# Router logits from the residual rows, two transposes in one go, VectorE for the first expert's low halves, and the first 256 tokens' branches inside the attention loop

## The chip, the cores and the metric

The kernel runs on one core of one Trainium2 chip. The metric is the device time of one execution in microseconds. Three executions of the kernel before took 3333.39, 3338.21 and 3341.09 us, median 3338.21 us. Line numbers of the kernel before are written as L and a number.

## The reference

One layer of an encoder for 2048 tokens of 1024 features, all in float32:

```
h   = rmsnorm(x, norm1_g);  P = h @ w_in           # columns: RWKV | attention q,k,v | two gates
y_A = RWKV7(forward + backward scan)               # 8 heads of 64, group norm, bonus term, times g
y_B = dilated window attention                     # 3 groups of 4 heads (dilation 1, 4, 16)
      # the groups are merged: o = sum_g softmax_g(lse) * o_g
x   = x + (sigmoid(g_A) * (y_A @ w_rwkv_out) + sigmoid(g_B) * (y_B @ w_attn_out)) @ w_out
h2  = rmsnorm(x, norm2_g)                          # x * rsqrt(mean(x*x) + eps) * norm2_g
grp = argmax(h2 @ w_router_group + b_router_group) # 4 groups of 8 experts
top 2 of (h2 @ w_router_expert + b_router_expert) inside grp; gate = p(grp) * softmax(top 2)
x   = x + sum over the 2 experts of gate * (silu(h2 @ w_gate) * (h2 @ w_up)) @ w_down
```

## The kernel before

The work is one straight program, in stages: projections; RWKV scans beside the rest of the projections; the windowed attention; a loop over eight blocks of 256 tokens that merges the two branches, projects, norms and routes; then the 32 experts; then a loop for what overflows an expert's slots. A framework plans the order of the instructions on each engine ahead of time, from its own estimates: work that stands earlier in the program goes first where it is ready, and later work fills gaps. On the chip each engine, and each queue of transfers, then runs its list strictly in that order. Tiles with one tag in a pool share that tag's buffers in turn, in program order; a pool that is closed gives its memory to the next.

Exact float32 products are made of two parts: a tile is split into a rounded high half (ScalarE copies it to `fp32r`) and the remainder (a subtraction), and three matmuls combine the halves (`PASS`).

**Attention** (L885 to L962). Three head groups, each with 16 tiles of 128 tokens, in the order 2, 1, 0. In a block of 2 or 4 tiles, q and k are loaded (`qkr`), transposed by TensorE into the PSUM tag `tq` of two banks, and copied out by VectorE (`KK`) and ScalarE (`QZ`). For each tile follow the scores (`s`), VectorE's mask and maximum (`sm`, `ob`), ScalarE's exponentials, a transpose (`pt`), the product with v (`po`) and a store of unnormed rows with their maxima and sums into the scratch tensor `o_d`. Each tile of groups 1 and 0 also advances `weights()`, which splits the weights of the next stage.

**Between** (L967 to L1036). Nine loads of constants into the pool `w5`: `gnB`, `g2`, `gup`, the router's weights `wr` (36 columns, in runs of 4 and 32 values) and biases `br`. Then `rwkv(0, psC, "tq")`. `rwkv(q)` finishes the RWKV branch of 256 tokens: it loads two scans' rows (`y0`, `y1`) and sums them, group norms them on VectorE, adds the bonus term with two steps on GpSimd (L1022, L1023), multiplies by the gate (two matmuls into PSUM, L1028, L1029), and `split_T` (L985 to L987) transposes the result and splits it to `yT`. It has three yields. Its PSUM tiles are those of the tag it is given.

**The block loop** (L1212 to L1246). `attn(q)` merges the three groups' rows: three loads of `oc` from `o_d`, small steps for the softmax over groups, a weighted sum (L1139 to L1141), `split_T` to `oT`. `attn(0)` stands ahead of the loop and takes its buffers from the pool `y5`, which opens after the attention's pools are closed. For each block q, `merge` runs 8 times (18 matmuls each into one of two banks `ab`, the gates `tg` loaded from scratch, a product on VectorE, then GpSimd and ScalarE); `residual` runs four times (two tiles of 128 tokens, two halves of 512 columns, 24 matmuls each into `px`); `norm2` squares on ScalarE, takes the inverse root with eleven small VectorE steps and scales (L1186); `logits` turns and multiplies for the router. The next block's `rwkv` and `attn` are advanced between these steps, with the PSUM tag `t5` of two banks. The second tile's logits and the routing (`tail`) are advanced in the next block, after merges 1, 3 and 5 and later.

`logits(h2, lg)` transposes four times into `th` (one bank), copies, runs four matmuls into `pl` (one bank), and then does all that again; between the halves it yields. `route` (L1056 to L1114) finds the group and the two experts, ranks the tokens of each expert and adds them to the table `ts`.

**The way to the experts** (L1248 to L1298). After the last block's routing, the experts are sorted by load (`order`), matmuls give the index tables (`IDX1`, `IDX2`), the pools are closed, and `load_gu(0, G)` loads the first expert's four pieces of 1 MB; `piece` lets ScalarE copy each half (L1288) and here GpSimd subtract (L1289), for all other experts VectorE. Then GpSimd gathers the first expert's rows (L1378).

Of the kernel before, what the change touches and what calls it, by code (L numbers as in the profile page):

```python
# [42 lines left out]
def hybrid_layer_kernel(ctx, tc, x, positions, norm1_g, w_in, mu_prev, mu_next, w_decay0, w_decay_up, a_gate0,  # L43
# [838 lines left out]
    made = 0  # L882
    wA, wB, wO = [], [], []
    parts_of_weights = weights()
    for g in (2, 1, 0):  # L885
# [4 lines left out]
        for i0 in range(0, NT, nb):  # L890
# [18 lines left out]
            for i in range(i0, i0 + nb):  # L909
# [57 lines left out]
    gnB = mk(w5, [128, 2, HD], F32, "gnB")  # L967
    nc.sync.dma_start(gnB[:, 0], gn_w[0:1, :].to_broadcast([128, HD]))
    nc.sync.dma_start(gnB[:, 1], gn_b[0:1, :].to_broadcast([128, HD]))
    g2 = mk(w5, [128, D], F32, "g2")  # L970
    nc.sync.dma_start(g2, norm2_g[0:1, :].to_broadcast([128, D]))
    gup = mk(w5, [128, HD], F32, "gup")
    nc.sync.dma_start(gup, g_up[0])
    wr = mk(w5, [128, KT, 36], F32, "wr")
    nc.sync.dma_start(wr[:, :, 0:4], w_router_group[0].rearrange("(k p) e -> p k e", p=128))
    nc.sync.dma_start(wr[:, :, 4:36], w_router_expert[0].rearrange("(k p) e -> p k e", p=128))
    br = mk(w5, [128, 36], F32, "br")
    nc.sync.dma_start(br[:, 0:4], b_router_group[0:1, :].to_broadcast([128, 4]))
    nc.sync.dma_start(br[:, 4:36], b_router_expert[0:1, :].to_broadcast([128, 32]))
    def split_T(dst, src, nk, ps, tag):  # L980

        for k in range(nk):
            pt = mk(ps, [128, 256], F32, tag)
            for j in range(2):
                PE.transpose(pt[:, j * 128:(j + 1) * 128], src[:, j, k * 128:(k + 1) * 128], ident)  # L985
            S.activation(dst[:, k, 0], pt, AF.Copy)
            V.tensor_tensor(dst[:, k, 1], pt, dst[:, k, 0], op=OP.subtract)  # L987

    def rwkv(q, ps, tag):

        tq = slice(q * 256, (q + 1) * 256)
        y0 = mk(yb, [128, 2, HD], F32, "y0")
        nc.sync.dma_start(y0, y_d[0, tq].rearrange("(j p) f -> p j f", p=128))
        y1 = mk(yb, [128, 2, HD], F32, "y1")
        nc.sync.dma_start(y1, y_d[1, tq].rearrange("(j p) f -> p j f", p=128))
        V.tensor_tensor(y0, y0, y1, op=OP.add)
        yh = y0.rearrange("p j (h n) -> p (j h) n", n=N)
        mu = mk(yb, [128, 16], F32, "mu")
        V.tensor_reduce(mu, yh, axis=AX.X, op=OP.add)
        V.tensor_scalar(mu, mu, 1.0 / N, None, op0=OP.mult)  # L1000
        V.tensor_tensor(yh, yh, mu[:, :, None].to_broadcast([128, 16, N]), op=OP.subtract)
        S.activation(y1, y0, AF.Square)
        yield
        V.tensor_reduce(mu, y1.rearrange("p j (h n) -> p (j h) n", n=N), axis=AX.X, op=OP.add)
        V.tensor_scalar(mu, mu, 1.0 / N, GN_EPS, op0=OP.mult, op1=OP.add)
        ri = mk(yb, [128, 16], F32, "ri5")
        rsqrt(yb, ri, mu, [128, 16], "rt5")
        V.tensor_tensor(yh, yh, ri[:, :, None].to_broadcast([128, 16, N]), op=OP.mult)
        V.tensor_tensor(y0, y0, gnB[:, 0, None, :].to_broadcast([128, 2, HD]), op=OP.mult)
        V.tensor_tensor(y0, y0, gnB[:, 1, None, :].to_broadcast([128, 2, HD]), op=OP.add)  # L1010
        yield
        vv = mk(yb, [128, 2, HD], F32, "y1")
        nc.sync.dma_start(vv, v_d[tq].rearrange("(j p) f -> p j f", p=128))
        vh = vv.rearrange("p j (h n) -> p j h n", n=N)
        bq = mk(yb, [2 * H, 256], F32, "bq")
        nc.sync.dma_start(bq, bon_d.rearrange("d h t -> (d h) t")[:, tq])
        pt = mk(ps, [128, 2, 2, H], F32, tag)
        for j in range(2):
            PE.transpose(pt[:, j].rearrange("p d h -> p (d h)"), bq[:, j * 128:(j + 1) * 128], ident[:2 * H, :2 * H])
        bsum = mk(yb, [128, 2, H], F32, "bsum")  # L1020
        V.tensor_reduce(bsum, pt.rearrange("p j d h -> p j h d"), axis=AX.X, op=OP.add)
        G.tensor_tensor(vh, vh, bsum[:, :, :, None].to_broadcast([128, 2, H, N]), op=OP.mult)  # L1022
        G.tensor_tensor(y0, y0, vv, op=OP.add)  # L1023
        sgt = mk(yb, [128, 256], F32, "sgt")
        nc.sync.dma_start(sgt, sg_d[:, tq])
        for j in range(2):
            pg = mk(ps, [128, HD], F32, tag)
            PE.matmul(pg, sgt[:, j * 128:(j + 1) * 128], gup, start=True, stop=True)  # L1028
            V.tensor_tensor(y0[:, j], y0[:, j], pg, op=OP.mult)  # L1029
        yield  # L1030
        yT = YT[q] = mk(yb, [128, 4, 2, 256], F32R, "yT")
        split_T(yT, y0, 4, ps, tag)

    YT, OT = {}, {}
    for _ in rwkv(0, psC, "tq"):
        pass  # L1036

    stC.close()

# [150 lines left out]
    def logits(h2, lg):  # L1190
        pl = mk(psE, [128, 36], F32, "pl", bufs=1)
        for k4 in range(2):
# [9 lines left out]
            if k4 == 0:  # L1202
                yield
# [8 lines left out]
    for _ in attn(0):  # L1212
        pass
# [382 lines left out]
```

## Time and profile before

| | |
|---|---|
| median of three runs | 3338.21 us |
| the profiled execution | 3351.28 us |
| its span, first to last instruction | 3349.6 us |
| mean granted clock of TensorE | 0.957 |
| attention | about 1820 to 2078 us |
| block loop, first merge to last residual | about 2079 to 2539 us |
| routing's end, index tables | about 2574 us |
| experts | about 2583 to 3336 us |

A row of a group of instructions gives line, engine, operation, output and input, count, then busy us, mean ns of one, and idle us of the engine ahead of them with what ended the idle time. A row of a timeline gives start and duration in us. PEld is TensorE's weight load, PEclk the granted clock as a share of full speed. TensorE's matmuls are pipelined, so their durations overlap.

### The profile page before, as it was taken

How to read it: one execution, taken by the hardware profiler on the slowest of the kernel's cores; microseconds unless marked ns; L12 is line 12 of the kernel's file. 1: busy time of each engine (PE TensorE's matmuls, PEld its weight loads, DVE VectorE, ACT ScalarE, POOL GpSimd, SP SyncE). 2: the span in 40 equal slices, each digit the busy share in tenths (PEclk: the TensorE clock that was granted, in tenths of full speed). 3: DMA queues.
4: the chain of work that ended last, by engine and by line, in shares of the span. 5: the costliest groups of instructions: out<-in, count | busy, mean ns of one | idle time of the engine just before them, and what ended most of it. 6: DMA issues, size and time to landing. Idle time of an engine off the chain costs nothing. (4 is left out here: it accounts for less than half of the span.)

```text
span 3349.6 us, 72079 instructions
## 1 busy us (share of the span) xinstructions
PE 3024.1 (90%) x29102; PEld 2466.8 (74%) x29102; DVE 2210.9 (66%) x4134; ACT 1522.0 (45%) x2913; POOL 544.8 (16%) x648
## 2 busy tenths in 40 slices
PE   6999978888989998898999987999996999999997
PEld 4888777667877787678877886778784667777775
DVE  5233368566766686648664776677774677888885
ACT  6333344453434434343433864111122566677764
POOL 0000012011112020112110000323233121222231
PEclk9899989999999999999999999999996999999999
DMA  7144365666545655565456654444433899999986
GB/s 280 60 136 137 98 208 194 211 199 206 161 150 174 201 167 160 166 199 162 145 172 184 182 174 144 129 130 144 127 120 115 286 308 323 337 336 341 330 295 201
DMA packets 361082, 652.63 MB, mean 195 GB/s; under 512 B 33717, under 2 KB 181765, under 8 KB 356522
## 3 DMA queue, kind: packets, MB, share of 16 engines
q1 hardware_dynamic: 338538, 599.61, 53.8%
q0 software_dynamic: 11104, 36.32, 4.4%
q10 hardware_dynamic: 11104, 12.06, 1.1%
q8 instruction: 230, 3.77, 0.5%
q14 instruction: 106, 0.87, 0.1%
HBM read 497.52 MB, written 153.10 MB: 194 GB/s over the span
## 5 line engine op out<-in xcount | busy, mean ns | idle before, releaser
L716 PE MATMUL dn<-wh,hk 128*128 128x256 f32 x3456 | 475.4, 295 | 24.0 <-DVE wh L659 9.4
L1289 DVE TENSOR_TENSOR wh<-raw,wh 128x1024 fp32r<-128x1024 f32 x376 | 441.4, 1219 | 80.1 <-ACT wh L1288 79.1
L716 PEld LDWEIGHTS dn<-wh,hk 128*128 128x128 f32 x3456 | 443.8, 200 | 42.5 <-DVE wh L659 11.1
L1288 ACT ACTIVATE wh<-raw 128x1024 fp32r<-128x1024 f32 x384 | 387.3, 1053 | 149.9 <-DMA raw<-in_w_down_dram 69.2
L720 PE MATMUL dn<-hk,wh 128*128 128x512 f32 x1536 | 404.1, 411 | 30.6 <-ACT gs L730 11.0
L1418 PE MATMUL pgu<-wh,xT 128*128 128x512 f32 x1536 | 377.7, 403 | 0.2 <-ACT xT L1393 0.2
L720 PEld LDWEIGHTS dn<-hk,wh 128*128 128x128 f32 x1536 | 284.5, 193 | 106.9 <-ACT gs L730 13.2
L1418 PEld LDWEIGHTS pgu<-wh,xT 128*128 128x128 f32 x1536 | 287.9, 190 | 78.1 <-issue 7.4
L280 PE MATMUL pp<-hq,wh 128*128 128x512 f32 x1008 | 254.0, 408 | 1.6 <-ACT hq L217 1.3
L280 PEld LDWEIGHTS pp<-hq,wh 128*128 128x128 f32 x1008 | 193.1, 194 | 48.0 <-ACT hq L217 2.3
L1174 PE MATMUL px<-w,mT 128*128 128x512 f32 x768 | 196.2, 406 | 0.0
L1462 PE MATMUL py<-wh,hT 128*128 128x512 f32 x768 | 191.4, 401 | 0.4 <-ACT hT L1440 0.4
L476 POOL TENSOR_TENSOR t<-t,ld 128x512 f32<-128x512 f32 x32 | 51.2, 1600 | 857.6 <-DVE t L465 483.9
L1174 PEld LDWEIGHTS px<-w,mT 128*128 128x128 f32 x768 | 142.8, 188 | 36.8 <-issue 3.4
L1462 PEld LDWEIGHTS py<-wh,hT 128*128 128x128 f32 x768 | 140.4, 188 | 33.1 <-issue 1.2
L1354 POOL DMA_INDIRECT out_dram<-ys,IDX x49 | 91.2, 1861 | 315.5 <-issue 105.5
L283 ACT ACTIVATE u<-pp 128x512 f32<-128x512 f32 x56 | 61.3, 1094 | 152.3 <-PE pp L280 125.3
L730 ACT ACTIVATE gs<-dn,drv 128x512 f32<-128x512 f32 x64 | 75.7, 1183 | 116.9 <-PE dn L720 80.5
L1158 PE MATMUL ab<-yT,w 128*128 128x256 f32 x768 | 114.4, 293 | 7.2 <-DVE tg L1161 3.6
L1378 POOL DMA_INDIRECT xg<-h_d,IDX x49 | 72.7, 1484 | 280.2 <-PE tx L1392 175.1
L1158 PEld LDWEIGHTS ab<-yT,w 128*128 128x128 f32 x768 | 99.5, 193 | 12.4 <-DVE tg L1161 5.6
L415 ACT ACTIVATE uv<-pre 32x512 f32<-32x512 f32 x128 | 75.2, 588 | 61.1 <-PE pre L409 59.9
(415 smaller groups left out, 5434.5 us busy)
## 6 DMA issues: line engine op xcount, KB each, us to landing
wh<-wc_d SPq DMA_DIRECT2D x204, 512.0 KB
raw<-in_w_gate_dram SPq DMA_DIRECT2D x64, 1024.0 KB
raw<-in_w_up_dram SPq DMA_DIRECT2D x64, 1024.0 KB
raw<-in_w_down_dram SPq DMA_DIRECT2D x64, 1024.0 KB
wc_d<-wh SPq DMA_DIRECT2D x68, 512.0 KB
ld<-rkk_d SPq DMA_DIRECT2D x192, 128.0 KB
raw<-in_w_in_dram SPq DMA_DIRECT2D x82, 256.0 KB
g_d<-gs SPq DMA_DIRECT2D x64, 256.0 KB
```

The source lines that it names most:

```text
L280: PE.matmul(pp, whs[k // 4][:, a, k % 4], hq[q][k // 2][:, k % 2, b], start=n == 0, stop=n == 3 * KT - 1)
L415: S.activation(uv[p * 64:p * 64 + 32, s::2].rearrange("p s (h e n) -> p s h e n", e=2, n=N)[:, :, :, e], pa[o:o + 32], AF.Copy)
L716: PE.matmul(pp[e][:, j * 256:(j + 1) * 256], lhs(2 * e + j, hk, k, a), wk_[:, b], start=k + j + m == 0, stop=k + j + m == KT + 2, skip_gro ...
L720: PE.matmul(pp[e], wk_[:, a, e * 128:e * 128 + 128], hk[k // 2][:, k % 2, b], start=k + m == 0, stop=k + m == KT + 1)
L730: S.activation(natural(gs), by_residue(pp[e]), AF.Tanh, scale=0.5, bias=DP[:, 38 + ct:39 + ct])
L1158: PE.matmul(pa[:, e], wt[k][:, a, cs_], src[:, k, b], start=e + n == 0, stop=n == 3 * nk - 1, skip_group_check=True)
L1174: PE.matmul(px, mT[k // 4][:, k % 4, a, j * 128:(j + 1) * 128], wO[k][:, b, fs], start=n == 0, stop=n == 3 * KT - 1)
L1288: S.activation(wh[:, 0, ks], raw[:, ks], AF.Copy)
L1289: eng.tensor_tensor(wh[:, 1, ks], raw[:, ks], wh[:, 0, ks], op=OP.subtract)
L1354: G.indirect_dma_start(out=x2_d, out_offset=bass.IndirectOffsetOnAxis(ap=idx, axis=0), in_=src, in_offset=None, bounds_check=T - 1, oob_is ...
L1418: PE.matmul(pgu[n], xT[:, x_, 4 * a + k], wh[:, w_, k], start=a + k + m == 0, stop=a + k + m == 6)
L1462: PE.matmul(py[f], hT[:, x_, 2 * a + k], wh[:, w_, k, f * 512:(f + 1) * 512], start=a + k + m == 0, stop=a + k + m == 4)
```

## The change

- The constants' loads, `split_T` and `rwkv` move ahead of the attention loop in the text. `wr` is multiplied by `norm2_g` once, with `norm2_g` loaded as `g2T` (1024 runs of one value).
- `rwkv(0)` and a new `attn0()` are advanced one step after each of the tiles 8 to 15 of the attention's last group. `attn0` does for 128 tokens at a time what `attn(0)` did for 256, in the buffers `y0` and `y1`; its transposes (`turn_o`) stay behind the attention.
- `logits` transposes `xr`, the residual rows, in two tiles of the tag `t5`, yields, and then runs the eight matmuls; the inverse root is multiplied in with the bias. The tag `th` is gone; `pl` has two banks.
- The first expert's subtractions are VectorE's.

```diff
+    wr = mk(w5, [128, KT, 36], F32, "wr")
...
+    g2T = mk(yb, [128, KT], F32, "bsum")
+    nc.sync.dma_start(g2T, norm2_g[0].rearrange("(k p) -> p k", p=128))
+    V.tensor_tensor(wr, wr, g2T[:, :, None].to_broadcast([128, KT, 36]), op=OP.mult)
...
+    def attn0():
+        for j in range(2):
+            oc = mk(yb, [128, 3, 264], F32, f"y{j}")
+            for g in range(3):
+                nc.sync.dma_start(oc[:, g], o_d[g, j * 128:(j + 1) * 128])
+            OC.append(oc)
+            yield
+            nm, sm = oc[:, :, 256:260], oc[:, :, 260:264]
+            mn = mk(yb, [128, 4], F32, "ri5")
...
+            V.tensor_tensor(og, og, wg[:, :, :, None].to_broadcast([128, 3, 4, N]), op=OP.mult)
+            V.tensor_tensor(oc[:, 0, 0:256], oc[:, 0, 0:256], oc[:, 1, 0:256], op=OP.add)
+            V.tensor_tensor(oc[:, 0, 0:256], oc[:, 0, 0:256], oc[:, 2, 0:256], op=OP.add)
+            yield
+    early = iter(())
     for g in (2, 1, 0):
...
                 if g < 2:
                     next(parts_of_weights, None)
+                if g == 0 and i >= 7:
+                    next(early, None)
+                    if i == 7:
+                        early = chain(rwkv(0, psC, "tq"), attn0())
...
-    for _ in rwkv(0, psC, "tq"):
+    for _ in early:
         pass
...
-        pr = mk(psE, [128, 2, 2, NE], F32, "pl", bufs=1)
+        pr = mk(psE, [128, 2, 2, NE], F32, "pl")
...
-    def logits(h2, lg):
-        pl = mk(psE, [128, 36], F32, "pl", bufs=1)
+    def logits(xr, r2, lg):
+        xT = []
         for k4 in range(2):
-            pt = mk(psE, [128, 4, 128], F32, "th", bufs=1)
+            pt = mk(psE, [128, 4, 128], F32, "t5")
             for k in range(4):
                 kk = k4 * 4 + k
-                PE.transpose(pt[:, k], h2[:, kk * 128:(kk + 1) * 128], ident)
-            hT = mk(y5, [128, 4, 128], F32, "h2T", bufs=2)
-            S.activation(hT, pt, AF.Copy)
-            for k in range(4):
-                kk = k4 * 4 + k
-                PE.matmul(pl, hT[:, k], wr[:, kk], start=kk == 0, stop=kk == KT - 1)
-            if k4 == 0:
-                yield
-        V.tensor_tensor(lg, pl, br, op=OP.add)
+                PE.transpose(pt[:, k], xr[:, kk * 128:(kk + 1) * 128], ident)
+            xT.append(mk(y5, [128, 4, 128], F32, "h2T", bufs=2))
+            S.activation(xT[k4], pt, AF.Copy)
+        yield
+        pl = mk(psE, [128, 36], F32, "pl")
+        for kk in range(KT):
+            PE.matmul(pl, xT[kk // 4][:, kk % 4], wr[:, kk], start=kk == 0, stop=kk == KT - 1)
+        V.scalar_tensor_tensor(lg, pl, r2, br, op0=OP.mult, op1=OP.add)
...
-    for _ in attn(0):
-        pass
+    turn_o(0, [oc[:, 0, 0:256] for oc in OC])
...
-            eng.tensor_tensor(wh[:, 1, ks], raw[:, ks], wh[:, 0, ks], op=OP.subtract)
+            V.tensor_tensor(wh[:, 1, ks], raw[:, ks], wh[:, 0, ks], op=OP.subtract)
...
-    wgu = load_gu(0, G)
+    wgu = load_gu(0)
```

## Rows read from the trace of the kernel before

**Rows 1.** The page: busy time by engine, and the main DMA queue.

```profile
PE 3024.1 (90%) x29102; PEld 2466.8 (74%) x29102; DVE 2210.9 (66%) x4134; ACT 1522.0 (45%) x2913; POOL 544.8 (16%) x648
...
q1 hardware_dynamic: 338538, 599.61, 53.8%
```

**Rows 2.** Busy time by stage: us, each engine, PEclk, DMA share, GB/s.

```profile
1975.00:2077.50 102.50, 92.45 (x694) 79.92 (x694) 62.80 (x98) 59.30 (x192) 4.25 (x2) 0.97 0.47 140
2077.50:2095.80 18.30, 5.39 (x34) 4.26 (x32) 12.64 (x34) 2.80 (x7) 0.00 (x0) 0.77 0.67 211
2095.80:2100.00 4.20, 4.16 (x15) 3.33 (x15) 3.75 (x5) 0.42 (x1) 1.57 (x2) 0.50 0.61 192
2100.00:2536.00 436.00, 404.09 (x2441) 342.52 (x2440) 306.54 (x907) 82.50 (x192) 139.94 (x141) 1.00 0.39 125
2538.50:2551.70 13.20, 5.90 (x25) 4.91 (x24) 3.95 (x15) 2.34 (x4) 0.00 (x0) 0.60 0.20 79
2551.70:2574.10 22.40, 5.71 (x18) 3.12 (x18) 17.48 (x59) 8.43 (x10) 9.29 (x4) 0.50 0.53 187
2610.00:3300.00 690.00, 684.37 (x3960) 494.95 (x3959) 548.50 (x590) 467.48 (x568) 147.67 (x86) 0.99 0.94 322
```

**Rows 3.** Timeline of TensorE behind the attention: start, us, instructions, idle before.

```profile
2078.95 3.13 PE L1158 MATMUL ab<-yT,w 128*128 128x256 f32 x24 [1.10 <-DVE yT L987]
2093.33 1.12 PE L985 MATMUL t<-ident,oc 128*128 128x128 f32 x4 [11.25 <-DVE oc L1141]
```

**Rows 4.** Timeline of the SyncE queue there.

```profile
2079.64 1.40 SPq L1122 DMA_DIRECT2D oc<-o_d  x3
2081.08 0.47 SPq L1152 DMA_DIRECT2D tg<-g_d  x1
```

**Rows 5.** Timeline of VectorE there, and shortly ahead of it.

```profile
2073.45 1.28 DVE L1029 TENSOR_TENSOR y<-y,tq 128x512 f32<-128x512 f32 x2 [2.30 <-POOL y L1023]
...
2089.99 1.83 DVE L1139 TENSOR_TENSOR oc<-oc,wg 128x768 f32<-128x768 f32 x2
...
2092.58 0.69 DVE L1141 TENSOR_TENSOR oc<-oc 128x512 f32<-128x512 f32 x1
```

**Rows 6.** TensorE's waits in the loop, 2097 to 2536 us: total, times, longest.

```profile
PE pl L1201 <- ACT h2T L1198: 10.3, 13, 1.5
PE th L1196 <- DVE h L1186: 8.6, 6, 1.4
```

**Rows 7.** Timeline of VectorE from the last residual to the index tables.

```profile
2538.61 0.69 DVE L1176 SCALAR_TENSOR_TENSOR xr<-px,xr 128x512 f32<-128x512 f32 x1 [4.57 <-PE px L1174]
...
2542.83 1.28 DVE L1186 SCALAR_TENSOR_TENSOR h<-xr,r,g 128x1024 f32<-128x1024 f32 x1
2551.62 0.20 DVE L1204 TENSOR_TENSOR LG<-pl,br 128x36 f32<-128x36 f32 x1 [7.50 <-PE pl L1201]
...
2573.88 0.19 DVE L1264 TENSOR_SCALAR IDX<-t 128x32 int32<-128x32 f32 x1 [1.37 <-PE t L1263]
```

**Rows 8.** Timeline of GpSimd at the attention's end.

```profile
2071.06 2.35 POOL L1023 TENSOR_TENSOR y<-y,y 128x1024 f32<-128x1024 f32 x1
```

**Rows 9.** Timeline of GpSimd there.

```profile
2558.68 9.29 POOL L1289 TENSOR_TENSOR wh<-raw,wh 128x1024 fp32r<-128x1024 f32 x4 [43.17 <-ACT wh L1288]
2574.97 1.19 POOL L1378 DMA_INDIRECT xg<-h_d,IDX  x1 [6.99 <-issue]
```

**Rows 10.** Groups of VectorE's instructions by form, 2550 to 2590 us.

```profile
L1112 DVE TENSOR_SCALAR rr<-io,RK 128x192 f32<-128x192 f32 x4 | 5.3, 1316 | 0.0
...
L1101 DVE TENSOR_TENSOR tm<-OH,io 128x64 f32<-128x64 f32 x2 | 4.5, 2286 | 0.0
...
L1101 DVE TENSOR_TENSOR tm<-OH,pk 128x64 f32<-128x64 f32 x2 | 0.4, 219 | 0.0
```

**Rows 11.** Groups of VectorE's instructions in the loop, 2078 to 2540 us.

```profile
L1112 DVE TENSOR_SCALAR rr<-io,RK 128x192 f32<-128x192 f32 x28 | 8.6, 309 | 0.0
```

**Rows 12.** Groups of VectorE's instructions by form, 2586 to 2700 us.

```profile
L1289 DVE TENSOR_TENSOR wh<-raw,wh 128x1024 fp32r<-128x1024 f32 x49 | 57.9, 1224 | 17.1 <-ACT wh L1288 16.8
```

More of the change, by code (lines that the diff above doesn't have):

```diff
@@ new lines, in attn0 @@
+    def attn0():
+        for j in range(2):
+            oc = mk(yb, [128, 3, 264], F32, f"y{j}")
+            for g in range(3):
+                nc.sync.dma_start(oc[:, g], o_d[g, j * 128:(j + 1) * 128])
+            OC.append(oc)
+            yield
+            nm, sm = oc[:, :, 256:260], oc[:, :, 260:264]
+            mn = mk(yb, [128, 4], F32, "ri5")
+            V.tensor_tensor(mn, nm[:, 0], nm[:, 1], op=OP.min)
+            V.tensor_tensor(mn, mn, nm[:, 2], op=OP.min)
+            wg = mk(yb, [128, 3, 4], F32, "mu")
+            V.tensor_tensor(wg, mn[:, None, :].to_broadcast([128, 3, 4]), nm, op=OP.subtract)
+            S.activation(wg, wg, AF.Exp)
+            V.tensor_tensor(sm, sm, wg, op=OP.mult)
+            den = mk(yb, [128, 4], F32, "bsum")
+            V.tensor_tensor(den, sm[:, 0], sm[:, 1], op=OP.add)
+            V.tensor_tensor(den, den, sm[:, 2], op=OP.add)
+            V.reciprocal(den, den)
+            V.tensor_tensor(wg, wg, den[:, None, :].to_broadcast([128, 3, 4]), op=OP.mult)
+            og = oc[:, :, 0:256].rearrange("p g (h n) -> p g h n", n=N)
+            V.tensor_tensor(og, og, wg[:, :, :, None].to_broadcast([128, 3, 4, N]), op=OP.mult)
+            V.tensor_tensor(oc[:, 0, 0:256], oc[:, 0, 0:256], oc[:, 1, 0:256], op=OP.add)
+            V.tensor_tensor(oc[:, 0, 0:256], oc[:, 0, 0:256], oc[:, 2, 0:256], op=OP.add)
+            yield
@@ L980, in split_T @@
[L980 to L1002, printed above, removed]
-        yield
[L1004 to L1032, printed above, removed]
@@ L1142, in attn, with turn_o @@
         yield
-        oT = OT[q] = mk(y5, [128, 2, 2, 256], F32R, "oT")
-        split_T(oT, oc[:, :, 0, 0:256], 2, psE, "t5")
+        turn_o(q, [oc[:, j, 0, 0:256] for j in range(2)])
+    def turn_o(q, src):
+        OT[q] = mk(y5, [128, 2, 2, 256], F32R, "oT")
+        split_T(OT[q], src, 2, psE, "t5")
     def merge(q, ct, mT):
@@ L1237, in hybrid_layer_kernel @@
             pass
-        for _ in logits(h2, LG[:, 0]):
+        for _ in logits(xr[0], r2, LG[:, 0]):
             pass
@@ L1243, in hybrid_layer_kernel @@
             pass
-        late = tail(q, LG, norm2(2 * q + 1, xr[1]))
+        late = tail(q, LG, xr[1], norm2(2 * q + 1, xr[1]))
     for _ in late:
@@ L1288, in piece, with load_gu @@
             S.activation(wh[:, 0, ks], raw[:, ks], AF.Copy)
[L1289 removed]
+            V.tensor_tensor(wh[:, 1, ks], raw[:, ks], wh[:, 0, ks], op=OP.subtract)
         return raw, wh
[L1292 to L1293 removed]
+    def load_gu(e):
+        return [piece(w, e, a, 4, 512) for a in range(2) for w in (w_gate, w_up)]
     def load_dn(e):
         return [piece(w_down, e, a, 2, 1024) for a in range(2)]
[L1298 removed]
+    wgu = load_gu(0)
     def overflow_list():
```

89 lines of the change are left out of this document (66 added, 23 removed).

## The prediction

> **What bounds the kernel now.** I read the page first: TensorE is busy for 3024.1 of 3349.6 us [rows 1], so time can only be won where it stands idle or waits. The table of stages [rows 2] shows where. In the last part of the attention (1975 to 2077.5 us) TensorE works 92.45 of 102.50 us. Then come 18.30 us with 5.39 us of TensorE work, then 4.20 us at a granted clock of 0.50, then the merge and projection loop with 404.09 of 436.00 us. From 2538.5 us the routing follows: 13.20 and 22.40 us with about 5.8 us of TensorE work each. After that the experts run, and TensorE is busy 684.37 of 690 us there [rows 2]; nothing in the change touches their steady state, so they begin earlier or later as a block. So the change is judged in four places: the attention, the hole behind it, the loop, the routing.
>
> The hole: TensorE does the first 24 merge matmuls at 2078.95 us and then waits 11.25 us for attn(0)'s sum [rows 3]. That chain starts late: its three loads issue at 2079.64 us, when the attention's buffers are free [rows 4], and the VectorE steps end at 2092.58 + 0.69 us [rows 5]. In the loop the waits of TensorE name the router: 10.3 us for the evicted transposes and 8.6 us for the normed rows [rows 6]. In the routing the order of VectorE's rows tells it: last residual at 2538.61, normed rows at 2542.83, logits only at 2551.62, index tables at 2573.88 us [rows 7].
>
> **The change, part by part.** The profiled execution took 3351.28 us, its span 3349.6; the median of the runs is 3338.21, 13.1 us (0.4%) lower. I work out differences on the profiled one and set them against the median.
>
> 1. *attn(0) in the attention.* It leaves the hole and gets buffers (y0, y1 of rwkv) that exist during the attention. If it is ready in time, the 18.30 us need only their 34 matmuls: 5.39 us at a clock of 0.77, some 4.2 us at full clock; 14 us less. The next 4.20 us at 0.50 [rows 2] are work for 2.1; 2 us less. Next late are the gates' loads: in the same queue they issue from 2081.08 us [rows 4], behind the three oc loads of 1.40 us that stay only for the second block. They can issue at about 2079.7, and with two banks for the merge sums TensorE runs out of work after those 24 matmuls (3.13 us), at some 2081; a load needs about 2 us (the program's first, issued at 0.80 us, was waited for until 2.9), and VectorE then frees a bank. 2 to 3 us of waiting stay. Gain 13 (6 to 16).
>
> 2. *What that costs inside the attention.* rwkv(0) already ran in the attention, but its part in the PSUM tag "tq" came behind the last transposes there: GpSimd's second step at 2071.06 us [rows 8], then VectorE waits 2.30 us for it [rows 5]. Now it stands behind tile 10 of 16 in program order, and the transposes of tiles 12 and 13 must wait for the same two banks until split_T is done. In the trace that stretch runs from bq's transposes at 2067.5 us to 2078.9, 11.4 us, against two tiles' own time: eight pairs in 102.5 us, 12.8 us a pair. So it nearly fits; what doesn't is 0 to 5 us. attn(0) adds, for each of two tiles, a product of 0.92 us, two sums of half of 0.69 us and nine steps of about 0.17: 3.1 us, 6.3 in all, on a VectorE that is busy 62.80 of 102.50 us [rows 2, 5]. The six loads take 2.8 us of the queue. Behind a stalled VectorE stand KK copies and masks, and TensorE waits for these. Loss 4 (0 to 10); nothing below zero, since nothing leaves that stage.
>
> 3. *Constants loaded ahead of the attention, wr times g2T.* The loads (nine, now ten) were hidden in the attention before, between other loads. New is that VectorE has to multiply wr by g2T, and everything behind it on VectorE waits for three loads of 1024 short pieces each. No row shows their landing. Below: nothing, if the multiply is placed late. Above: the main queue spent 53.8% of 16 engines' span on 338538 packets [rows 1], 85 ns a packet; 3072 packets on 16 engines are 16 us. Part of it lies beside the start of the attention. I take 4 (0 to 14), nearer to nothing, since the first attention loads wait for other things too.
> The Trainium skill (DMA: Bandwidth & Descriptors, Bandwidth) puts a packet at about 10.5 ns and calls small transfers descriptor-dominated: for g2T's 1024 pieces alone an estimate of 10.8 us. By it the forecast would be some 7 us later; it is the third rival below.
>
> 4. *Router in the loop.* Transposes start from the residual, not from the normed rows, so the 8.6 us for L1186 fall away except for the 0.69 us of the residual step itself, which is then next. Both groups of four are transposed ahead of the eight matmuls, so TensorE no longer stops for each copy; in the late half the matmuls stand two merge steps behind. That is up to 18.9 us [rows 6]. But the transposes now use "t5", whose two banks hold rwkv's gate products until GpSimd and VectorE are through (2.35 us and more [rows 8]); the former bank of their own is gone. If each of seven blocks waits as long as that, 16 us come back. The matmuls, copies and the one step for the logits are as many as before. Gain 12 (2 to 19).
>
> 5. *The last logits.* Now: residual until 2539.30, square and rsqrt until 2542.8, normed rows until 2544.11, then two rounds of transpose, copy, matmul until 2551.6 [rows 7]. After: the transposes run beside the square; the copies (0.6 us each) come behind it on ScalarE, at 2540.5; the matmuls end at 2543 to 2545, when the root is there too. Logits at about 2544.5: gain 7 (5 to 8). The first expert's loads, which issue when the logits have been read, come forward with it.
>
> 6. *First expert's subtractions by VectorE.* GpSimd does eight, 2.3 us each, four of them from 2558.68 on [rows 9]. In that time VectorE's small steps swell: four steps L1112 take 5.3 us, where 28 in the loop have a mean of 309 ns; two of L1101 4.5 us, where their like take 0.4 [rows 10, 11]. 4.1 + 4.1 = 8.2 us of the 22.3 from logits to tables. That goes. In its place VectorE does eight steps of 1.224 us [rows 12], 9.8 us; they are free to slip into the route's chain wherever it pauses, and the pauses for TensorE hide some 2.5 us. If six come ahead of the tables: 7.3 - 2.5 = 4.8 lost; if none, 0; if all and VectorE has to wait for their raw rows too, 11. Gain 8.2 - 3.2 = 5 (+9 to a loss of 3). The first gather stands directly behind the tables (2574.97 us [rows 9]), so this is worth its full time.
>
> Sum: -13 + 4 + 4 - 12 - 7 - 5 = -29 us; 3338.2 - 29 = 3309.
>
> **Rivals.** *The loop's wait only changes its name*: for "t5" instead of for the normed rows. For it: the rows of GpSimd lie just where the transposes would go. Against: in the loop the old transposes came some 3 us behind the gate products' use anyway. Part 4 shrinks to 2: 3319. *Subtractions in the way*: VectorE takes instructions in order, and one that waits for its raw half holds the route; part 6 turns to +3: 3317. *The constants' multiply stalls the start*: part 3 costs 14: 3319. *The attention is stretched, slower than before*: eight tiles get one step each, and each step puts VectorE or the load queue behind something slower (two loads from scratch, GpSimd's 4.3 us, a square on ScalarE, three loads that may have to wait for the store just issued). The gains outside the attention are 37 - 4 = 33 us, so it decides from 4.1 us a step on; at 5 us: 3345. Against it: VectorE has 40% to spare there, and the steps are independent of the tiles but for the two banks. *It doesn't do what it says*: instructions run in an order that was planned ahead, not as written (rwkv(0)'s first sums were at 1824 us); if attn(0)'s rows still come last, the hole keeps 8 us: 3317.
>
> **How the numbers follow.** Forecast 55% (its own range 3297 to 3322), t5 13%, subtractions 8%, multiply 9%, attn(0) late 7%, stretched attention 8%. All but the last end below; adding two or three of the middle ones brings the time near 3331 and into no change. A difference of 0.2%, 6.7 us, is what can be told from none. Faster 84%, the same 8%, slower 8%. Range 3291 to 3334: beyond its upper end lies the stretched attention, below its lower end all gains at their best.
>
> **What would show it.** Right: behind the attention no wait for oc and a clock near 1.00; TensorE's waits in the loop without L1186 and with little for the transposes' copies; logits 5 us behind the last residual instead of 13; L1112 and L1101 at 0.3 us throughout; no subtraction on GpSimd. Wrong: an attention over 8 us longer than now (258 us from the first transposes at 1820.2 us to the last at 2077.9); VectorE idle at its start for wr; new waits for "t5"; subtractions between logits and tables with waits for ScalarE before them; the experts taking another time than now.

## The result: slower, by the blocks of the loop

The changed kernel takes 3359.28 us (median of 5 runs, 3358.80 to 3366.82), the kernel before 3338.21 (3333.01 to 3344.03) beside it: ratio 1.0063, 95% interval 1.0045 to 1.0080. The forecast was 3309 us. The profiled execution took 3358.8 us, its span 3357.0; that of before had 3351.28, which is 13 us above its median, so the two profiles differ by only 7.4 us where the medians differ by 21. What follows compares stages. One execution of e_comb3 below, of 7178.87 us, was slow and is left out of its median.

TensorE is busy 20 us longer than in [rows 1], by the page of after:

```profile
PE 3044.2 (91%) x29102; PEld 2484.5 (74%) x29102; DVE 2217.9 (66%) x4153; ACT 1522.1 (45%) x2914; POOL 524.4 (16%) x640
```

with as many instructions. Its busy time by stage (columns as in [rows 2]):

```profile
1980.00:2083.00 103.00, 88.29 (x599) 77.62 (x598) 59.60 (x108) 52.35 (x167) 4.26 (x2) 0.87 0.39 117
2083.00:2087.30 4.30, 4.18 (x22) 4.18 (x23) 0.76 (x2) 0.72 (x3) 0.00 (x0) 0.58 0.61 171
2100.00:2560.00 460.00, 413.97 (x2383) 347.50 (x2382) 318.18 (x914) 80.91 (x189) 140.81 (x135) 0.96 0.37 120
2561.00:2566.80 5.80, 3.08 (x24) 2.58 (x22) 3.91 (x15) 2.12 (x4) 0.00 (x0) 0.80 0.22 90
2566.80:2583.70 16.90, 5.44 (x18) 3.24 (x18) 14.78 (x64) 8.43 (x10) 0.00 (x0) 0.50 0.78 279
2610.00:3300.00 690.00, 684.13 (x3975) 494.46 (x3977) 550.00 (x590) 468.30 (x569) 141.25 (x87) 1.00 0.95 324
```

Against [rows 2]: the hole is 4.3 us and full of work, the two routing stages are 5.8 and 16.9 us in place of 13.2 and 22.4, the experts are the same. But the attention's end runs at a granted clock of 0.87 (it was 0.97), and the loop is longer: from the first merge with oT to the last residual it takes 473.7 us, where it took 444.0. TensorE's waits in it (total, times, longest), which answer [rows 6]:

```profile
PE ab L1198 <- DVE tg L1201: 11.9, 10, 1.8
PE px L1214 <- ACT mT L1204: 11.0, 7, 2.9
PE pl L1149 <- DVE OW L1145: 10.5, 6, 1.8
PE t L905 <- DVE oT L907: 5.6, 7, 0.8
PE px L1214 <- POOL mT L1205: 3.8, 6, 0.6
```

The waits for h (8.6 us) and h2T (10.3 us) are gone, as meant. In their place stand OW, tg and mT. Before, mT was not among the waits, and the other two were short:

```profile
PE ab L1158 <- DVE tg L1161: 3.6, 7, 0.8
PE pl L1113 <- DVE OW L1109: 1.3, 6, 0.2
```

One block of the loop on TensorE (start, us, instructions, idle before):

```profile
2247.22 0.87 PE L1238 MATMUL t<-ident,xr 128*128 128x128 f32 x6
2249.85 1.01 PE L1149 MATMUL pl<-rr,OW 128*64 128x192 f32 x4 [1.76 <-DVE OW L1145]
2251.28 1.76 PE L1244 MATMUL pl<-wr,h2T 128*128 128x36 f32 x8
2255.40 7.76 PE L1214 MATMUL px<-w,mT 128*128 128x512 f32 x22
2263.01 0.60 PE L905 MATMUL t<-ident,oc 128*128 128x128 f32 x4
```

and the windows over it:

```profile
2248.00:2252.00 4.00, 2.24 (x12) 1.67 (x11) 2.38 (x7) 0.99 (x2) 0.00 (x0) 0.80 0.32 131
2252.00:2256.00 4.00, 4.00 (x17) 3.71 (x18) 0.26 (x1) 0.18 (x1) 0.00 (x0) 0.50 0.39 131
```

OW, the routing's last product of the block before, stands behind h2's scaling on VectorE:

```profile
2247.41 1.28 DVE L1227 SCALAR_TENSOR_TENSOR h<-xr,r,g 128x1024 f32<-128x1024 f32 x1
2249.45 0.35 DVE L1145 TENSOR_TENSOR OW<-OH,TW 128x64 f32<-128x64 f32 x2
```

So the wait kept its end and changed its name. Behind it, in this block, the granted clock goes from 1.00 to 0.50, from 2.4 to 1.2 GHz, for some 10 us: eight logit products take 1.76 us, and from the second group of rr's products to the transposes of oc pass 13.2 us. The wait comes in six blocks, which have the same instructions in the same order. Four others are followed by a fall of some 7 us, and the sixth by none; there the eight products take 0.98 us and the stretch to the transposes of oc 8.5 us, as before the change:

```profile
2500.72 0.86 PE L1149 MATMUL pl<-rr,OW 128*64 128x192 f32 x4 [1.75 <-DVE OW L1145]
```

```profile
2501.00:2505.00 4.00, 4.00 (x29) 3.44 (x28) 0.60 (x2) 0.60 (x1) 0.00 (x0) 1.00 0.58 199
```

**An account.** I cut the loop into pieces of 2 us; idle is the span less TensorE's busy time, and what the clock costs is the sum of busy time x (1 - granted clock). The rest is work at full clock.

| profiled execution | loop us | idle | clock | work | attention us (first to last po) | idle | clock | work |
|---|---|---|---|---|---|---|---|---|
| before | 444.0 | 32.4 | 4.6 | 407.0 | 243.7 | 21.6 | 5.7 | 216.3 |
| after | 473.7 | 46.1 | 20.3 | 407.3 | 258.4 | 25.1 | 15.2 | 218.0 |

In the loop the work is the same, with 13.7 us more of waiting and 15.7 more for the low clock. These are single executions. Two kernels below whose engines have the same order of instructions in the loop, e_early and e_oldrouter, have 36.0 and 36.3 us of waiting there, but 8.6 and 16.5 for the clock; so up to about half of the 15.7 us can belong to the execution. That the clock is lower in the changed kernel holds over the runs: its five have a mean granted clock of 0.950 to 0.954, the 33 of the kernel before beside e_sub one of 0.954 to 0.960.

### The profile page after: what moved, and what is told of

Read it like the earlier page. It is cut to its first block, busy times and chain, and to the rows that moved or that the text cites. A ratio compares the mean times of both kernels' runs of the same rounds, so it can differ in the third digit from the quotient of the medians.

```text
span 3357.0 us, 72104 instructions
## 1 busy us (share of the span) xinstructions
PE 3044.2 (91%) x29102; PEld 2484.5 (74%) x29102; DVE 2217.9 (66%) x4153; ACT 1522.1 (45%) x2914; POOL 524.4 (16%) x640
## 5 line engine op out<-in xcount | busy, mean ns | idle before, releaser
L1329 DVE TENSOR_TENSOR wh<-raw,wh 128x1024 fp32r<-128x1024 f32 x384 | 451.5, 1220 | 78.7 <-ACT wh L1328 77.7
L716 PEld LDWEIGHTS dn<-wh,hk 128*128 128x128 f32 x3456 | 442.2, 199 | 42.2 <-DVE wh L659 11.1
L1214 PE MATMUL px<-w,mT 128*128 128x512 f32 x768 | 207.7, 424 | 14.9 <-ACT mT L1204 11.0
L1214 PEld LDWEIGHTS px<-w,mT 128*128 128x128 f32 x768 | 150.0, 200 | 58.6 <-ACT mT L1204 13.9
L1198 PEld LDWEIGHTS ab<-yT,w 128*128 128x128 f32 x768 | 97.7, 191 | 21.6 <-DVE tg L1201 16.8
L1418 POOL DMA_INDIRECT xg<-h_d,IDX x49 | 58.5, 1195 | 341.3 <-PE tx L1432 186.4
L1202 POOL TENSOR_TENSOR tg<-tg 128x256 f32<-128x256 f32 x64 | 62.2, 972 | 270.1 <-DVE tg L1201 246.0
```

The source lines that it names most:

```text
L716: PE.matmul(pp[e][:, j * 256:(j + 1) * 256], lhs(2 * e + j, hk, k, a), wk_[:, b], start=k + j + m == 0, stop=k + j + m == KT + 2, skip_gro ...
L1198: PE.matmul(pa[:, e], wt[k][:, a, cs_], src[:, k, b], start=e + n == 0, stop=n == 3 * nk - 1, skip_group_check=True)
L1202: G.tensor_tensor(tg[:, 0], tg[:, 0], tg[:, 1], op=OP.add)
L1214: PE.matmul(px, mT[k // 4][:, k % 4, a, j * 128:(j + 1) * 128], wO[k][:, b, fs], start=n == 0, stop=n == 3 * KT - 1)
L1329: V.tensor_tensor(wh[:, 1, ks], raw[:, ks], wh[:, 0, ks], op=OP.subtract)
```

## The experiments

All times are medians, with the ratio to the kernel before, run beside each on the same chip, and its 95% interval. Not all ran on the same chip, so two experiments are compared by their ratios. A difference in us to the kernel before is the ratio's share of its time. "Hole" is the time from the attention's last po to the first merge with oT; "idle" and "clock" are the columns of the account above, from each run's profile.

**Parts alone.** Four kernels split the change.

*e_sub*: before, the subtractions alone.

```diff
-    wgu = load_gu(0, G)
+    wgu = load_gu(0)
```

> The kernel before with one edit alone: the subtractions that make the low halves of the first expert's gate and up weights are VectorE's in place of GpSimd's. Theory (the change lost in the loop of the blocks, its other parts came out as reckoned): this part gives what the profile after shows between the last logits and the list of indices, 22.3 us before against 16.8 after, so about 3333 against 3338, 5 us less. Rival: the shorter stretch after came from the other parts (GpSimd freed, logits earlier), then this kernel stands within 2 us of before, or is slower where the eight subtractions get in the way of the routing on VectorE.

Measured: 3338.86, 0.9981 (0.9966 to 0.9996), 6 us less. From logits to index tables 18.7 us in place of 22.4. The small steps no longer swell: the same four steps that took 1316 ns each in [rows 10] here:

```profile
L1112 DVE TENSOR_SCALAR rr<-io,RK 128x192 f32<-128x192 f32 x4 | 1.2, 313 | 0.0
```

*e_router*: before, the router alone (the diff's `logits`, `tail`, banks, and `wr` times `g2T`).

> The kernel before with the router's change alone: logits from the rows not yet normed, transposes in two banks, norm2's gain multiplied into the router's weights. Theory (the router's part cost the time): the loop is some 25 to 30 us longer and the last logits come 7 us earlier, so about 3338 + 21 = 3359, as slow as the whole change or slower. Rival (the blocks are longer since TensorE, VectorE and ScalarE enter them some 12 us earlier or with another order of the first merge, not for the router): 3331 to 3338, no slower than before.

Measured: 3358.96, 1.0048 (1.0032 to 1.0064), 16 us more, as the theory had it. The loop takes 467.8 us (idle 39.9, clock 21.6), and the logits come 5.7 us behind the last residual.

*e_early*: before, the branches in the attention alone (constants ahead, `rwkv(0)` and `attn0` stepped, `turn_o`).

> The kernel before with the first 256 tokens' branches inside the attention alone: constants loaded ahead of the attention, rwkv(0) and the attention's merge for the first tokens a step at a time from the seventh subtile of the last group, router and first expert as before. Theory: the hole behind the attention shrinks by 12 us and the attention itself grows by 10, so 3336 against 3338, within 5 us of it. Rival (the stretched attention is an accident of that profile, or belongs to the gain's multiply): 3325, 13 us less. Rival (entering the loop early is what lengthens its blocks): slower, 3350 or more.

Measured: 3359.06, 1.0039 (1.0027 to 1.0052), 13 us more. The hole is 5.7 us in place of 17.5, but from first to last po pass 266.5 us (clock 23.0) against 243.7. The attention takes more than the hole yields, and the loop is 7 us longer besides (451.2, of which the clock is 4.0 more). This is a miss for the theory, which had this part near zero; the time is that of the last rival.

*e_oldrouter*: the changed kernel with the router of before.

> The changed kernel with the router put back as it was (logits from the normed rows in two rounds with one bank, no gain in the router's weights); the branches inside the attention and the first expert's subtractions on VectorE stay. Theory (router's part is the only loss): 12 us less in the hole, 10 more in the attention, 5 less behind the loop, so about 3331 against 3338, and 28 us under the changed kernel. Rival (the parts lose together, not the router alone): above 3345.

Measured: 3352.67, 1.0027 (1.0015 to 1.0038), 9 us more: above what the theory allowed, and near what e_early and e_sub add up to (13 - 6). The parts add, within intervals of some 5 us each: 16 + 13 - 6 = 23 for the 21 measured. So there are two losses, not one.

**The loop.** *e_routefirst*: the changed kernel with the rest of the routing ahead of norm2.

```diff
+        for _ in late:
+            pass
         r2 = norm2(2 * q, xr[0])
         next(nA, None)
         residual(xr[1], mT, 1, 0)
-        for _ in late:
-            pass
```

> The changed kernel with one thing moved: the rest of the routing of the block before (the two products of rr with OW) is issued ahead of norm2 of the block's first tile instead of behind it, so that TensorE needs OW in the middle of the second residual product and VectorE makes it before it scales h2. Theory A (each block of the changed kernel loses 4.7 us since TensorE waits 1.76 us in one piece for OW behind h2's scaling and runs at a granted clock of 0.50 for some 10 us after it): the wait goes, the clock holds at 1.00, a block takes 57 instead of 62 us in six or seven blocks, 3359 less some 28 to 33 = 3326 to 3331. Theory B (the loss is in the merges, where TensorE waits for tg and mT, VectorE's and GpSimd's and ScalarE's steps, 3.3 us a block): no gain, 3355 to 3360. Theory C (the clock falls at any short wait in the block, wherever it is): the wait turns up elsewhere, 3350 to 3360.

Measured: 3367.28, 1.0067 (1.0049 to 1.0085). Theory A's gain did not come; the wait turned up earlier, as C had it: "PE pl L1149 <- DVE rr L1148" has 12.9 us in 6 waits. But the clock's cost fell to 8.1 us while idle rose to 50.4, which is not what C said of the clock, and the time is above all three ranges.

*e_rounds*: two rounds and banks as before, the rows not yet normed.

```diff
+        pl = mk(psE, [128, 36], F32, "pl", bufs=1)
...
-            pt = mk(psE, [128, 4, 128], F32, "t5")
+            pt = mk(psE, [128, 4, 128], F32, "th", bufs=1)
...
-        yield
-        pl = mk(psE, [128, 36], F32, "pl")
-        for kk in range(KT):
-            PE.matmul(pl, xT[kk // 4][:, kk % 4], ...)
+            for k in range(4):
+                kk = k4 * 4 + k
+                PE.matmul(pl, hT[:, k], ...)
```

> The changed kernel with the logits still from the rows not yet normed, but in the two rounds of before: four transposes, one copy, four products, with one bank of their own and the products' bank no longer double. Theory A (the order that the planner writes around the wait for OW makes the loss): less of it, as the order around OW comes out another way, 3330 to 3350; what remains is read from the granted clock behind OW. Rival B (taking the rows not yet normed is the loss, since the transposes come at another point of the block): 3355 to 3360. Rival C (the two transposes' turn in the banks that oT and yT also use is the loss): 3335 or less, with no wait for OW needed.

Measured: 3339.93, 0.9980 (0.9966 to 0.9995). B falls. The time is in A's range, but the wait for OW is still 10.4 us, so it is not what the gain on the changed kernel went by (0.8% by the ratios, some 28 us): the waits for ScalarE's mT and for tg fell (first fence below), and the clock's cost to 13.4 us; 6.2 us of waits for h2T are back with the two rounds. C's ground is nearest, though its 3335 was not reached.

*e_t5rounds*: those two rounds with the change's banks.

```diff
-        pl = mk(psE, [128, 36], F32, "pl", bufs=1)
+        pl = mk(psE, [128, 36], F32, "pl")
...
-            pt = mk(psE, [128, 4, 128], F32, "th", bufs=1)
+            pt = mk(psE, [128, 4, 128], F32, "t5")
```

> The changed kernel with the logits in two rounds (four transposes, a copy, four products, twice) but with the banks of the change: the transposes share their two banks with oT and yT, the products' bank is double. Against the kernel with two rounds and a bank of its own, which came out at 0.998 of before, this tells the banks from the grouping. If the grouping of the eight transposes and eight products is the loss: 3338 to 3345. If the banks are: 3355 to 3365.

Measured: 3369.20, 1.0083 (1.0064 to 1.0101): the banks, not the grouping. Two things about banks went together here, the transposes' share of `t5` and the second bank of `pl`; they were not tried apart. TensorE's waits in the loop of e_rounds, then of e_t5rounds (the waits for oT, 2.6 and 5.6 us, for h2T, 6.2 and 9.2, and for GpSimd's mT, 4.5 and 3.8, are left out):

```profile
PE pl L1149 <- DVE OW L1145: 10.4, 6, 1.7
PE px L1214 <- ACT mT L1204: 2.9, 1, 2.9
...
PE ab L1198 <- DVE tg L1201: 2.4, 3, 1.8
```

```profile
PE px L1214 <- ACT mT L1204: 11.0, 7, 2.9
PE pl L1149 <- DVE OW L1145: 10.5, 6, 1.8
...
PE ab L1198 <- DVE tg L1201: 3.8, 7, 1.8
```

*e_fill*: the changed kernel, the first tile's transposes three times each.

```diff
-            for k in range(4):
+            for k in list(range(4)) * n:
```

> The changed kernel with useless work added: the eight transposes of the first tile's rows are done three times each, 16 more a block for TensorE, 128 in all, some 0.14 us each. Theory A (the clock falls because TensorE stands still for 1.76 us there): TensorE does 2.2 us more where it waited anyway, the granted clock holds in most blocks, and the kernel is faster by 10 to 28 us though it does more: 3331 to 3349. Theory B (the wait itself or the merges are the loss, and the clock goes its own way): 2.2 us more a block less what fits into the wait, 3360 to 3375.

Measured: 3366.47, 1.0078 (1.0063 to 1.0093), a miss for A's time and inside B's. The added transposes came behind the wait, not into it, so their 2 us a block were paid in full (work 422.1 us in the loop, 15 more). The clock held better, as A had it (cost 8.3 us in place of 20.3; mean granted clock 0.952 to 0.957 in its six runs). A block of it on TensorE:

```profile
2255.63 0.86 PE L1149 MATMUL pl<-rr,OW 128*64 128x192 f32 x4 [1.74 <-DVE OW L1145]
2256.43 2.18 PE L1238 MATMUL t<-ident,xr 128*128 128x128 f32 x18
2258.45 0.98 PE L1244 MATMUL pl<-wr,h2T 128*128 128x36 f32 x8
```

*e_routelate*: the changed kernel with the rest of the routing behind the last residual.

```diff
         residual(xr[1], mT, 1, 0)
-        for _ in late:
-            pass
...
         residual(xr[1], mT, 1, 1)
+        for _ in late:
+            pass
```

> The changed kernel with the rest of the routing of the block before moved the other way: issued behind the block's last residual instead of ahead of the logits, so that the products of rr with OW stand behind the second residual product on TensorE and nothing near the logits waits for VectorE. Theory A (a wait of 1.7 to 2.2 us behind the first residual product, whatever it is for, is what the granted clock falls after, and the fall costs 4.6 us a block): no wait there, clock 1.00 to the end of the block, 57 us or less a block in place of 62, 3359 less about 30 = 3329. Theory B (the merges' waits for tg and mT are the loss): 3355 to 3360. If the wait for OW now stands ahead of the transposes of oc, the loss is there: 3345 or more.

Measured: 3328.45, 0.9953 (0.9940 to 0.9965), 1.1% less than the changed kernel by the ratios, some 37 us (the medians, of two chips, are 31 apart), as theory A put it. The loop takes 437.2 us (idle 26.8, clock 3.3, against 46.1 and 20.3), and the wait for OW is not in the list any more:

```profile
PE px L1214 <- ACT mT L1204: 7.3, 7, 2.9
PE ab L1198 <- DVE tg L1201: 7.1, 10, 1.8
```

**The attention.** *e_attn*: before, with the attention's merge for the first tokens alone in the attention, stepped from the ninth tile of the last group, its rows in the buffers of `g2` and `yT`; `rwkv(0)` as before.

```diff
+                if g == 0 and i >= 8:
+                    next(early, None)
...
-    for _ in attn(0):
-        pass
+    turn_o(0, OC)
```

> The kernel before with the attention's merge for the first 256 tokens alone done a step at a time from the ninth subtile of the last group (norm2's gain is loaded a little later, to make room); rwkv(0) stays behind the attention as before. Theory A (what stretches the attention by 10 to 20 us is rwkv(0)'s steps in it, whose sums on VectorE stand ahead of the attention's tb and whose transposes wait for y): the attention keeps its 244 to 247 us, the hole shrinks from 17.5 to 5 us or less, 3338 less 12 = 3326. Rival B (any step in the attention stretches it): the attention grows by as much as the hole shrinks, 3335 to 3345. Rival C (the hole is then ended by rwkv(0) or by loads, not by oT): hole 10 us or more, 3333.

Measured: 3347.78, 0.9999 (0.9982 to 1.0016): no gain, as rival B had it. The hole is 3.7 us, but from first to last po pass 254.7 us, with 12.5 for the clock. The other branch, rwkv(0)'s steps, was not tried alone.

*e_best1*: that, the subtractions, and the new logits for the last tile only.

> The parts that gained, without the two that lost: the kernel before with the attention's merge for the first tokens alone in the attention, the first expert's subtractions by VectorE, and the logits from the rows not yet normed for the last tile only (norm2's gain multiplied into the router's weights once, in the last block). Theory (the gains add: 12 in the hole, 5 before the list of indices, 7 behind the last residual, and the loop keeps its 444 to 448 us): 3338 less 24 = 3314. Rival (entering the loop earlier lengthens it, as with both branches in the attention, where the loop came out at 451 and 459 us): 3320 to 3330. Below both kernels in either case.

Measured: 3338.26, 0.9975 (0.9960 to 0.9989), 8 us where 24 were expected. In its profile the blocks, from last residual to last residual, take 56.9, 56.8, 61.5, 61.6, 61.5, 61.5 us. The first and the third have the same instructions in the same order on four engines, with the same wait for h, 1.58 us in both, and 5.0 us idle in both; the clock costs 0.0 us in the one and 5.1 in the other. Windows of 3 us from that wait on, in the one and in the other:

```profile
2189.00:2192.00 3.00, 1.42 (x9) 0.85 (x7) 2.83 (x9) 0.00 (x1) 0.00 (x0) 1.00 0.16 63
2192.00:2195.00 3.00, 2.80 (x20) 2.25 (x20) 0.86 (x5) 1.20 (x2) 0.00 (x0) 1.00 0.98 341
...
2302.70:2305.70 3.00, 1.38 (x9) 0.71 (x6) 2.86 (x9) 0.18 (x1) 0.00 (x0) 1.00 0.11 42
2305.70:2308.70 3.00, 2.84 (x13) 2.33 (x13) 0.69 (x3) 1.01 (x2) 0.00 (x0) 0.64 0.96 325
```

**Versions that beat both.** *e_comb*: before, changed router, subtractions, rest of the routing late, nothing in the attention.

> The kernel before with the changed router, the first expert's subtractions by VectorE and the rest of the routing behind the block's last residual, and with neither of the first tokens' branches in the attention. Theory A: attention and hole as before, blocks of 57 us or less without a fall of the clock, 7 us less behind the last residual, 5 less before the list of indices: 3338 - 12 = 3326, below both kernels, and less where the waits for h and h2T that are gone shorten the blocks as well (2.4 us each, 19 in all: 3307). Theory B: blocks of 61 to 62 us as with the router's change alone, 3338 + 16 - 5 = 3349.

Measured: 3320.43, 0.9931 (0.9917 to 0.9945), as theory A had it. The loop takes 432.6 us, with idle 21.5 and clock 4.8.

*e_late*: the same with the old router.

> The kernel before, its old router (logits from the normed rows), with the first expert's subtractions by VectorE and the rest of the routing moved behind the block's last residual: the same as the best kernel so far without the changed router. Theory (the move gains only where the logits don't wait for the normed rows): TensorE now waits for the normed rows the 0.9 us longer that the two products of rr took, 2.4 us in one piece in every block, and the granted clock falls behind it: 6 us more of waits and up to 17 more at a low clock, 3333 + 6 to 23 = 3339 to 3356. Rival (the move alone is the gain, and the changed router with it gives nothing): 3320 or less.

Measured: 3347.98, 1.0017 (0.9996 to 1.0037). The time is in the theory's range. The move alone gives nothing, and rather costs: e_sub, which lacks it, has 0.9981. With the changed router it gives 1.1% (e_routelate). But the theory's fall of the clock behind every wait for h did not come: of the six waits, of 2.2 to 2.3 us, four were followed by no fall and two by one of 3.4 us (clock in the loop 6.9). One of the four, and windows behind it and behind one of the two:

```profile
2246.63 0.66 PE L1196 MATMUL th<-ident,h 128*128 128x128 f32 x4 [2.24 <-DVE h L1186]
```

```profile
2246.60:2250.00 3.40, 3.37 (x23) 2.94 (x24) 0.58 (x1) 0.92 (x2) 0.00 (x0) 1.00 0.77 253
2187.40:2190.60 3.20, 3.02 (x11) 2.64 (x11) 0.73 (x2) 0.60 (x1) 0.00 (x0) 0.50 0.71 237
```

*e_comb2*: e_comb with two rounds and the transposes in a bank of their own.

> The best kernel so far (before, changed router, rest of the routing late, first expert's subtractions by VectorE) with the logits in two rounds and the transposes in a bank of their own. The two kernels with two rounds and with the wait for OW in place came out 29 us apart by their banks alone. Theory (the banks matter by themselves: with shared ones the second tile's transposes come later, beside the merges, where TensorE then waits for mT and oT): idle time under 21 us, 3310 or less. Rival (they mattered only through where the wait for OW fell): the same as the best so far, 3316 to 3324.

Measured: 3311.28, 0.9894 (0.9875 to 0.9912), the fastest. The loop takes 423.1 us, with idle 14.2 and clock 7.9. So the banks and rounds matter also where no wait for OW is left; rounds, `t5` and the one bank of `pl` were changed together here. TensorE between two blocks, here and in e_comb:

```profile
2251.49 0.66 PE L988 MATMUL t<-ident,oc 128*128 128x128 f32 x4
2251.99 0.38 PE L1200 MATMUL th<-ident,xr 128*128 128x128 f32 x2
2252.30 0.86 PE L1116 MATMUL pl<-rr,OW 128*64 128x192 f32 x4
...
2254.03 0.41 PE L988 MATMUL t<-ident,y 128*128 128x128 f32 x2 [0.49 <-DVE oT L990]
2254.28 0.86 PE L1205 MATMUL pl<-wr,h2T 128*128 128x36 f32 x6
```

```profile
2249.14 0.66 PE L988 MATMUL t<-ident,oc 128*128 128x128 f32 x4
...
2251.46 0.74 PE L988 MATMUL t<-ident,y 128*128 128x128 f32 x4 [0.86 <-DVE oT L990]
...
2257.50 1.04 PE L1200 MATMUL t<-ident,xr 128*128 128x128 f32 x8
```

With a bank of its own the second tile's router work fills the gap behind oc's transposes. In the banks that oc and y use its transposes come 8.4 us behind oc's, not 0.5, between the merges, and TensorE waits for tg and mT instead (4.7 and 8.5 us in the loop; 2.6 and none here).

*e_comb3*: e_comb and e_attn together.

> The best kernel so far with the attention's merge for the first 256 tokens in the attention (rwkv(0) behind it as before). Theory (the hole's 13 us are got back at some 8 to 10 us more of attention, half of it at a lower granted clock): 3320 less 3 to 5 = 3315 to 3317. Rival (with the waits in the blocks gone, nothing of the earlier start is lost, and the attention's growth belongs to single executions): 3308. Rival (the start of the loop at another time brings falls of the clock back into the blocks): 3325 or more.

Measured: 3319.15, 0.9931 (0.9913 to 0.9950), the ratio of e_comb; none of the three expectations had this time. The branch in the attention is worth nothing here either.

## Why the prediction was wrong, point by point

The items below are differences of two profiles. They close: -12.4 + 9.9 + 29.7 - 7.3 - 5.5 is 14.4; the attention began 4.8 us earlier and the stretch behind the index tables was 2.2 shorter, which leaves the 7.4 us between the spans.

1. *attn(0) leaves the hole, 13.* Right. The hole, 17.5 us to the first merge with oT, is 5.1 (12.4 less); the matmuls run through:

```profile
2083.89 3.59 PE L1198 MATMUL ab<-yT,w 128*128 128x256 f32 x18
2087.31 0.28 PE L1198 MATMUL ab<-oT,w 128*128 128x256 f32 x1
```

2. *Its cost in the attention, 4 (0 to 10).* Too small, and the second step that failed. From its first transposes the attention takes 266.8 us in place of 256.9, 9.9 more, and in e_early, where items 1 and 2 stand without the router and the subtractions, they lost 13 us net where the sum had a gain of 9. What I sized was time on VectorE; not in the sum was the clock, 9.5 of the account's 14.7 us. Waits are 3.5 of them: TensorE waits 4.9 us for VectorE's tb (1.1 before) and 9.1 for ScalarE's sm (6.6 before). Over the profiles the clock costs 1.7 to 11.1 us in the attentions without a branch (six of them), 6.7 to 14.3 with the attention's merge alone (three), 10.2 to 24.7 with both (eight).

3. *Constants and wr times g2T, 4 (0 to 14).* Nothing. VectorE reaches the multiply at 1828.57 us and doesn't stand idle for it:

```profile
1828.57 0.46 DVE L895 TENSOR_TENSOR wr<-wr,bsum 128x288 f32<-128x288 f32 x1
```

The loads were issued at 1802.7 us (g2T), 1820.9 and 1821.9 us (wr). The short pieces took far less than either price in the prediction. In the 2 us from 1804 on the queues moved as many small packets as g2T has pieces (57 in the 2 us before):

```profile
DMA packets 1215, 0.35 MB, mean 175 GB/s; under 512 B 1046, under 2 KB 1046, under 8 KB 1215
```

In the 4 us from 1825 on they moved 2241 under 512 bytes, for wr's 2048. That is about 2 ns a packet on all engines together, where the prediction's 85 ns on one of 16 engines makes 5.3. The estimate of 10.8 us for g2T from the Trainium skill (DMA: Bandwidth & Descriptors, Bandwidth) is not borne out: by these counts its pieces had moved some 3 us after their issue.

4. *Router in the loop, 12 gained.* The failing step: 29.7 us lost in the profiles, and 16 of the 21 by e_router alone, with the 7 us of item 5 already taken off. Two things in it were wrong. "The 8.6 us fall away except for the residual step, which is then next" looked only at the chain of the logits. But just there stood in TensorE's order the products of rr with OW, whose VectorE steps come behind h2's scaling: next was OW, at the same point of the block, for 1.76 us in place of h's 1.44. Moving them away (e_routelate) gave some 37 us. And the price of the shared banks was put as a wait for "t5" of 2.35 us; no such wait appeared (the one that names these banks, for oT, is 5.6 us as before). The banks cost by order, as far as the timelines show: in e_comb the second tile's transposes land between merges, and in e_comb2 they fill a gap. Giving them a bank of their own, with `pl` back to one bank, was worth 1.0% (e_t5rounds against e_rounds). The clock was not in the sum of this step either. With both mended, and the logits in two rounds again, the router is worth some 35 us less time together with the subtractions (e_comb2), so the idea of the step was right, its place among the others not.

5. *Last logits, 7.* Right, 7.3: 13.0 to 5.7 us. The logits' step still stands behind the normed rows on VectorE, but nothing else comes between, where 7.50 us of waiting for TensorE stood before [rows 7]:

```profile
2565.46 1.28 DVE L1227 SCALAR_TENSOR_TENSOR h<-xr,r,g 128x1024 f32<-128x1024 f32 x1
2566.66 0.25 DVE L1245 SCALAR_TENSOR_TENSOR LG<-pl,r,br 128x36 f32<-128x36 f32 x1
```

6. *Subtractions, 5.* Right, 5.5 in the profile and 6 alone. Of the ten subtractions on VectorE from 2560 to 2600 us five fell ahead of the tables, 1.22 us each, near the six of the estimate.

Rivals: "the loop's wait only changes its name" was the nearest, with the wrong name (t5 for OW) and a quarter of the price (10 us where the step missed by 42), since the clock was not in it. The stretched attention cost 1.2 us a step (9.9 over 8; 2.9 in e_early), under its 4.1. No rival had the loop itself slower, which is where the sign came from.

## What to carry to other kernels

Before a wait is taken away from an in-order engine, list what stands in its queue at that point and ask of each item where its producer stands: the end of the wait may be held by a second item that hides behind the first. A shared buffer can cost places and not only waits: work that could fill a gap is planned elsewhere. Where the clock can halve, a short wait can cost more than its length, and the cost varies: here one wait of 1.76 us was followed by 4.7 us more for the same work, and a wait of 1.75 us in another block by none. A profile of one execution can't tell such a cost from luck; several runs with their granted clocks can.

## What the runs showed of the hardware

- The granted clock is not set by the instruction stream alone. In e_best1 the same wait of 1.58 us with the same work around it left the clock at 1.00 in one block and at 0.50 for some 10 us in another, at 4.6 us. Four waits of 2.2 us in e_late left it at 1.00; five of six of 1.76 us in the changed kernel did not. The kernel before, e_sub and e_late have the same order of instructions through the attention, on TensorE, VectorE and GpSimd without exception: it takes 243.7, 247.4 and 239.7 us, with 21.0 to 21.6 us idle in each and 5.7, 11.2 and 1.7 for the clock. The Trainium skill (TensorE: Matmul & The Clock Gate, HAM oscillation) tells of a kernel whose wait in every tile lets the clock fall in every tile; the changed kernel is near that, with a fall behind five of its six waits for OW, but its sixth and the traces of e_late and e_best1 show that it need not. What else decides is open. The spread between executions goes with it: of the kernel before in 33 runs (3331.55 to 3351.55 us), the eight fastest have a mean granted clock of 0.958 to 0.960, the eight slowest one of 0.954 to 0.957.
- VectorE's small steps swell beside GpSimd's subtractions: of the same form one takes 1316 ns on average in the stretch where GpSimd was busy for 9.29 of 22.40 us, and 313 ns without them (e_sub).
- Loads of many short pieces were quick: 1046 packets under 512 bytes moved in 2 us (the changed kernel, 1804 to 1806 us).
